# A channel shuffle in 24-row tiles: stores issued in turn by ScalarE and GpSimd, copies on VectorE alone, small tiles at both ends

## The chip, the cores and the metric

One core of a Trainium2 chip. The experiments ran in five sessions, on chips 1, 3, 12 and 13, and each ratio is against the kernel before as run in the same session. The time is device microseconds (us) of one execution, and medians are given with the lowest and highest of all executions of that kernel on the chip at hand.

## The reference

The input `x` is float32 of shape 16 x 64 x 64 x 256. The 256 channels of each pixel are 8 groups of 32, and the result has the two axes exchanged: output channel `i*8 + g` is input channel `g*32 + i`. Nothing is computed; 67.11 MB are read and 67.11 MB written.

```python
x = x.reshape(batch, h, w, groups, channels_per_group)
x = x.transpose(0, 1, 2, 4, 3)
x = x.reshape(batch, h, w, c)
```

## The kernel before

The pixels are a list of 65,536 rows of 256 floats. A tile holds 24 rows on each of 128 partitions (24 KB a partition, 3 MB in all); there are 21 such tiles and one of 8 rows. Each is loaded from SyncE's queue, permuted inside each partition by two strided copies (first half of the rows on VectorE, second on ScalarE), and stored from ScalarE's queue. Four input and four output buffers let the stages overlap; a scheduler decides the order on each engine.

```python
_SIZES = [24] * 21 + [8]
_IN_BUFS = 4
_OUT_BUFS = 4
_SHARES = (("vector", 1), ("scalar", 1))
# ... cut: rows() takes q rows for each of 128 partitions; permute() is one strided copy
    first = 0
    for q in _SIZES:
        in_tile = in_pool.tile([P, biggest * c], F32, name="in_tile")
        nc.sync.dma_start(out=in_tile[:, : q * c], in_=rows(x_flat, first, q))
        out_tile = out_pool.tile([P, biggest * c], F32, name="out_tile")
        at, total = 0, sum(n for _, n in _SHARES)
        for k, (engine, n) in enumerate(_SHARES):
            # ... cut: the engine's share of the rows, at to upto
                permute(engine, out_tile[:, cols], in_tile[:, cols])
        nc.scalar.dma_start(out=rows(out_flat, first, q), in_=out_tile[:, : q * c])
        first += P * q
```

Of the kernel before, what the change touches and what calls it, by code (L numbers as in the profile page):

```python
# [1 line left out]

# [4 lines left out]


F32 = mybir.dt.float32
P = 128  # L10

_SIZES = [24] * 21 + [8]
_IN_BUFS = 4
_OUT_BUFS = 4

_SHARES = (("vector", 1), ("scalar", 1))


@with_exitstack
def kernel(  # L20
    ctx: ExitStack,
    tc: tile.TileContext,
    x: bass.AP,
    groups: bass.AP,
    out: bass.AP,
):
    nc = tc.nc
    b, h, w, c = x.shape
    G = int(groups)
    CPG = c // G  # L30
    assert G * CPG == c
    assert sum(_SIZES) * P == b * h * w
    biggest = max(_SIZES)

    x_flat = x.rearrange("b h w c -> (b h w c)")
    out_flat = out.rearrange("b h w c -> (b h w c)")

    in_pool = ctx.enter_context(tc.tile_pool(name="in_pool", bufs=_IN_BUFS))
    out_pool = ctx.enter_context(tc.tile_pool(name="out_pool", bufs=_OUT_BUFS))

    def rows(flat, first, q):

        return flat[first * c : (first + P * q) * c].rearrange("(p f) -> p f", p=P)

    def permute(engine, dst, src):
        src = src.rearrange("p (i g j) -> p i j g", g=G, j=CPG)
        dst = dst.rearrange("p (i j g) -> p i j g", j=CPG, g=G)
        if engine == "scalar":
            nc.scalar.copy(out=dst, in_=src)  # L49
        else:  # L50
            getattr(nc, engine).tensor_copy(out=dst, in_=src)  # L51

    first = 0
    for q in _SIZES:
        in_tile = in_pool.tile([P, biggest * c], F32, name="in_tile")
        nc.sync.dma_start(out=in_tile[:, : q * c], in_=rows(x_flat, first, q))
        out_tile = out_pool.tile([P, biggest * c], F32, name="out_tile")
        at, total = 0, sum(n for _, n in _SHARES)
        for k, (engine, n) in enumerate(_SHARES):
            last = k == len(_SHARES) - 1  # L60
            upto = q if last else min(q, at + -(-q * n // total))
            if upto > at:
                cols = slice(at * c, upto * c)
                permute(engine, out_tile[:, cols], in_tile[:, cols])
            at = upto
        nc.scalar.dma_start(out=rows(out_flat, first, q), in_=out_tile[:, : q * c])  # L66
        first += P * q


# [1 line left out]
_INS = ['x', 'groups']  # L71
_OUTS = [((16, 64, 64, 256), 'float32')]

_NUMBERS = {'groups': 8}


# [26 lines left out]
```

## Time and profile before

| | before |
|---|---|
| time, median (lowest to highest) | 317.53 us (317.53 to 317.59, 3 runs) |
| span of the profiled run | 316.0 us |
| DMA engines' time: loads, stores | 49.8%, 49.3% |
| start of one tile's copy to the next, 103.62 to 292.64 us | 14.54 us (13 steps) |

The page of the profile opens with the busy time of each engine. In its strip each digit is the busy share, in tenths, of one fortieth of the span (7.9 us here); the GB/s line says what the DMA engines moved in it. Then come the DMA queues (q1 is SyncE's, q10 ScalarE's) and the costliest groups of instructions, with the idle time before them and who ended it.

```profile
span 316.0 us, 236 instructions
DVE 65.3 (21%) x22; ACT 118.9 (38%) x23; POOL 0.2 (0%) x4
...
DMA  8999999999999999999999999999999999999996
GB/s 302 439 395 426 426 445 432 420 442 439 417 439 445 417 436 442 426 426 445 426 423 445 439 414 442 442 417 439 442 421 432 442 420 432 442 429 429 421 446 291
...
q1 hardware_dynamic: 3168, 67.11, 49.8%
q10 hardware_dynamic: 3168, 67.11, 49.3%
...
L49 ACT COPY out_tile<-in_tile 128x3072 f32<-128x3072 f32 (+1 forms) x22 | 117.7, 5348 | 184.6 <-DMA in_tile<-in_x_dram 184.6
L51 DVE COPY out_tile<-in_tile 128x3072 f32<-128x3072 f32 (+1 forms) x22 | 65.3, 2968 | 238.3 <-DMA in_tile<-in_x_dram 238.3
```

The two queues add up to 99.1% of the time of all sixteen DMA engines, and both copying engines spend most of the span waiting for loads. The kernel is bound by DMA; only the first and the last slice are short. The windows view of the same run says it by stretch. Its columns are the stretch, its length, the busy us of VectorE, ScalarE and GpSimd (with their instructions), the granted clock, the DMA share and the GB/s; rows left out are marked by dots.

```profile
100.00:150.00 50.00, 11.83 (x4) 19.12 (x4) 0.00 (x0) 1.00 1.00 433
200.00:250.00 50.00, 9.90 (x4) 17.29 (x4) 0.00 (x0) 1.00 1.00 432
...
300.00:308.00 8.00, 1.09 (x1) 1.94 (x1) 0.00 (x0) 1.00 1.03 443
308.00:314.00 6.00, 0.00 (x0) 0.00 (x0) 0.00 (x0) 1.00 0.90 382
314.00:316.00 2.00, 0.00 (x0) 0.00 (x0) 0.00 (x0) 1.00 0.01 4
```

So about 433 GB/s is held to 308 us, and 382 from there to 314. 134.22 MB at 433 GB/s are 310.0 us. The timeline shows why the end is full: when the last small load lands at 302.35, two stores (4 MB, 9.7 us of DMA) are still to be made.

```profile
292.64 5.43 ACT L49 COPY out_tile<-in_tile 128x3072 f32<-128x3072 f32 x1 [9.11 <-DMA in_tile<-in_x_dram]
...
302.35 1.94 ACT L49 COPY out_tile<-in_tile 128x1024 f32<-128x1024 f32 x1 [4.29 <-DMA in_tile<-in_x_dram]
302.41 2.25 ACTq L66 DMA_DIRECT2D out_dram<-out_tile  x2
```

### The profile page before, as it was taken

The page shows a single profiled execution, that of the slowest core. Times are in us where ns is not written, and L with a number is a line of the kernel's source. Part 1 is how long each engine was busy: PE and PEld are TensorE (multiplying, and loading weights), DVE is VectorE, ACT ScalarE, POOL GpSimd, SP SyncE. Part 2 cuts the span into 40 slices and gives each one's busy share as a digit, 9 for nine tenths or more (in the row PEclk, how much of TensorE's full clock was granted, in tenths as well). Part 3 has the DMA queues.
Part 4 walks back from the last instruction along what each step waited for, and adds up shares of the span by engine and source line. Part 5 has one row for each costly group of instructions (what it writes and reads, how often), then busy time and mean ns, then how long its engine had stood idle before and what let it go on. Part 6 is the DMA issues. An engine that isn't in the chain of part 4 may idle for free.

```text
span 316.0 us, 236 instructions
## 1 busy us (share of the span) xinstructions
DVE 65.3 (21%) x22; ACT 118.9 (38%) x23; POOL 0.2 (0%) x4
## 2 busy tenths in 40 slices
DVE  0440321303030303113030303031220303030310
ACT  1681624425160606243351606061533426060620
POOL 0000000000000000000000000000000000000000
DMA  8999999999999999999999999999999999999996
GB/s 302 439 395 426 426 445 432 420 442 439 417 439 445 417 436 442 426 426 445 426 423 445 439 414 442 442 417 439 442 421 432 442 420 432 442 429 429 421 446 291
DMA packets 6337, 134.23 MB, mean 425 GB/s; under 512 B 704, under 2 KB 704, under 8 KB 704
## 3 DMA queue, kind: packets, MB, share of 16 engines
q1 hardware_dynamic: 3168, 67.11, 49.8%
q10 hardware_dynamic: 3168, 67.11, 49.3%
q14 instruction: 1, 0.01, 0.0%
HBM read 67.11 MB, written 67.11 MB: 425 GB/s over the span
## 4 chain that ended last, share of the span: by engine, by line
another core or an unknown queue 43%; DMA 32%; ACT 20%; ACTq 1%; issue 0%
DMA in_tile<-in_x_dram 32%; ACT out_tile L49 20%; ACTq L66 1%; ACTq L49 0%
## 5 line engine op out<-in xcount | busy, mean ns | idle before, releaser
L49 ACT COPY out_tile<-in_tile 128x3072 f32<-128x3072 f32 (+1 forms) x22 | 117.7, 5348 | 184.6 <-DMA in_tile<-in_x_dram 184.6
L51 DVE COPY out_tile<-in_tile 128x3072 f32<-128x3072 f32 (+1 forms) x22 | 65.3, 2968 | 238.3 <-DMA in_tile<-in_x_dram 238.3
L49 ACT ACT_TABLE_LOAD x1 | 1.3, 1283 | 0.7 <-PEq L84 0.7
L84 POOL MEMSET const-bfloat16-1.0<- 128x1 bf16 x1 | 0.1, 102 | 0.0
L84 POOL MEMSET const-uint8-127<- 128x1 uint8 x1 | 0.1, 102 | 0.0
L84 POOL MEMSET const-float32-1.0<- 128x1 f32 x1 | 0.1, 99 | 0.0
L84 POOL MEMSET const-float32-0.0<- 128x1 f32 x1 | 0.1, 98 | 0.2 <-issue 0.2
## 6 DMA issues: line engine op xcount, KB each, us to landing
in_tile<-in_x_dram SPq DMA_DIRECT2D x21, 3072.0 KB, 52.6
out_dram<-out_tile ACTq DMA_DIRECT2D x21, 3072.0 KB, 20.2
in_tile<-in_x_dram SPq DMA_DIRECT2D x1, 1024.0 KB, 47.9
out_dram<-out_tile ACTq DMA_DIRECT2D x1, 1024.0 KB, 10.4
```

Of the source, the lines that this page charges most:

```text
L49: nc.scalar.copy(out=dst, in_=src)
L51: getattr(nc, engine).tensor_copy(out=dst, in_=src)
L66: nc.scalar.dma_start(out=rows(out_flat, first, q), in_=out_tile[:, : q * c])
L84: nc = _bacc.Bacc("TRN2", target_bir_lowering=False, num_devices=1)
```

## The change

The intent: take the copies off ScalarE so that it need only issue stores; issue each store right after its copy, from two engines in turn; start and end with small tiles so that the pipeline fills and drains faster.

```diff
-_SIZES = [24] * 21 + [8]
+_SIZES = [8] + [24] * 20 + [8, 8, 8]
-_SHARES = (("vector", 1), ("scalar", 1))
+_SHARES = (("vector", 1),)
...
+    ctx.enter_context(tc.manual_schedule(engines=None))
     first = 0
-    for q in _SIZES:
+    for t, q in enumerate(_SIZES):
...
-        nc.scalar.dma_start(out=rows(out_flat, first, q), in_=out_tile[:, : q * c])
+        storer = (nc.scalar, nc.gpsimd)[t % 2]
+        storer.dma_start(out=rows(out_flat, first, q), in_=out_tile[:, : q * c])
```

## The prediction

> **What bounds the kernel now.** The 16 DMA engines. The strip of slices shows DMA at 9 tenths or more in 38 of 40 slices; the queue part gives 49.8% of the engines' span to loads and 49.3% to stores, 99.1% together. In steady state the timeline's copies start every 14.55 us; one tile loads and stores 6.29 MB, so 432.5 GB/s. 134.2 MB at that rate is 310.3 us, against a span of 316.0. Only about 5.7 us is left to win, all at the ends: slice 1 moved 302 GB/s and slice 40 moved 291. VectorE is 21% busy, ScalarE 38%; the groups by line show both waiting for loads (238 and 185 us). The chain of waits names ScalarE for 20%, but DMA never ran dry under it.
>
> **The change, costed.**
> 1. Copies. ScalarE loses 22 copies (5.51 us per 12 rows), VectorE doubles: 12 rows took 3.06 us, so 24 rows about 6.0 us (estimate), 8 rows 2.0. About 130 us busy in all, 6.0 of each 14.55. Off the critical path: 0.
> 2. Program order. Now stores go out in pairs: store 20 was issued at 302.4 us though its copies ended at 298.1. Afterwards each goes right after its copy. In steady state DMA has work anyway: 0.
> 3. Two store queues. The Trainium skill, "DMA: Bandwidth & Descriptors", section "Issuing engines are not separate DMA queues", says all issuers share the same 16 engines. At 99.1% busy this brings no bandwidth. I expect 14.5 to 14.6 us per tile again. A GpSimd store will start 0.5 to 2 us later than a ScalarE one (a guess; this trace has no GpSimd DMA). "SBUF — State Buffer" (box on the "DVE blocks DMA" trap) says descriptor writing is locked out while VectorE copies in a two-port mode. Here VectorE is idle 8.5 us of each 14.55, and a store is issued just when its copy has ended, so little should be lost.
> 4. Small first tile. The first store goes near 8.5 us, not 16.8. But four loads already fill DMA then: 0.
> 5. Three small last tiles. Here I expect a loss. Now the last small load took 9.7 us (292.6 to 302.35) beside a large store, four times its own 2.4 us: small rows share badly. At its landing about 4.2 MB of stores were still to go, and covered the last copy. Afterwards three small loads crawl beside two store queues that drain the backlog early. After the last landing come copy 2.0, issue 1.2 to 2.5, transfer 2.4, completion about 1.3 us, with only the store before (2.4 us) to cover copy and issue. DMA idle at the end: 1.5 to 4 us more.
>
> Sum: +1.5 to +4 us, perhaps one more if GpSimd's queue is costly: 317.5 becomes about 319.8 us, range 316.3 to 324.0. Faster by over 2% would need 311.2 us, which leaves no ends at all: 1%. Slower by over 2% needs the GpSimd queue to lower the steady rate: 11%. Within 2%: 88%.
>
> **What would show it.** Copy spacing 14.5 to 14.6 us; VectorE near 130 us busy; first slices as full as now; fewer GB/s in the last two slices, with a gap between the last load's landing and the last store, which GpSimd issues; the first GpSimd store landing later than a ScalarE one.
>
> **What would make it wrong.** GpSimd descriptors smaller than the rows (many more packets) or uneven over engines, lowering the rate below 430 GB/s; descriptor writing that waits for VectorE; or, to the good side, last stores still backed up when the last load lands, so that the end is no longer than now.

## The result

| | before | after |
|---|---|---|
| time, median (lowest to highest), 6 runs each | 317.56 us (317.53 to 317.80) | 326.15 us (325.18 to 327.88) |
| ratio after / before, 95% interval | | 1.0271 (1.0242 to 1.0300) |
| span of the profiled run | 316.0 us | 326.1 us |
| VectorE busy | 65.3 us | 121.8 us |
| start of one 24-row copy to the next, mean of 13 | 14.54 us | 14.97 us (100.35 to 294.95) |

A ratio is the mean time of one kernel's fast runs over that of the other's fast runs of the same rounds, so it is not quite the ratio of the medians quoted. The change is slower by 2.7%. The profiled execution after is the slowest of its six (327.88 us), so its span overstates the difference a little; the spread among runs, 2.7 us against 0.3 before, is itself new.

The page after, with the lines that answer to those of before (q0 is GpSimd's software queue):

```profile
span 326.1 us, 175 instructions
DVE 121.8 (37%) x24; POOL 6.7 (2%) x16
...
DMA  8999999999999999999999999999999999999953
GB/s 322 394 425 434 425 434 425 434 431 431 425 431 434 428 434 428 428 422 428 422 410 431 434 434 434 434 431 431 431 428 419 431 425 431 431 410 388 411 250 133
...
q1 hardware_dynamic: 3456, 67.11, 48.5%
q10 hardware_dynamic: 1728, 33.56, 24.2%
q0 software_dynamic: 1728, 33.56, 24.1%
...
L51 DVE COPY out_tile<-in_tile 128x6144 f32<-128x6144 f32 (+1 forms) x24 | 121.8, 5077 | 198.6 <-DMA in_tile<-in_x_dram 198.6
L68 POOL DMA_DIRECT2D out_dram<-out_tile x12 | 6.5, 543 | 314.3 <-DVE out_tile L51 314.3
```

VectorE still mostly waits for loads: it has not become the bound. The software queue moved as many packets as ScalarE's (1,728 each, the same bytes), so the rows were not cut smaller. What changed is the last two slices, 250 and 133 GB/s where before had 446 and 291, and a little less than 433 in many others. The windows view after has no column for ScalarE, which runs no copies any more:

```profile
100.00:150.00 50.00, 22.79 (x4) 1.06 (x2) 1.00 1.00 429
200.00:250.00 50.00, 18.39 (x4) 0.53 (x1) 1.00 1.00 428
250.00:290.00 40.00, 15.69 (x3) 1.06 (x2) 1.00 1.00 425
...
300.00:308.00 8.00, 2.71 (x3) 0.53 (x1) 1.00 0.92 390
308.00:314.00 6.00, 2.00 (x1) 0.00 (x0) 1.00 0.97 408
314.00:318.00 4.00, 0.00 (x0) 0.00 (x0) 1.00 0.20 86
318.00:322.00 4.00, 2.02 (x1) 0.53 (x1) 1.00 0.10 41
322.00:326.00 4.00, 0.00 (x0) 0.00 (x0) 1.00 0.56 229
```

From 314 to 322 us the DMA share is 0.2 and then 0.1: about three, then fewer than two of sixteen engines at work on average. The timeline of that stretch shows what everybody was waiting for:

```profile
294.95 5.68 DVE L51 COPY out_tile<-in_tile 128x6144 f32<-128x6144 f32 x1 [8.01 <-DMA in_tile<-in_x_dram]
...
302.80 2.05 DVE L51 COPY out_tile<-in_tile 128x2048 f32<-128x2048 f32 x1 [2.17 <-DMA in_tile<-in_x_dram]
...
307.97 2.02 DVE L51 COPY out_tile<-in_tile 128x2048 f32<-128x2048 f32 x1 [3.12 <-DMA in_tile<-in_x_dram]
318.38 2.02 DVE L51 COPY out_tile<-in_tile 128x2048 f32<-128x2048 f32 x1 [8.38 <-DMA in_tile<-in_x_dram]
320.69 0.53 POOL L68 DMA_DIRECT2D out_dram<-out_tile  x1 [15.01 <-DVE out_tile L51]
```

The last load, 1 MB, landed 10.4 us after the one ahead of it, though DMA was nearly idle for the last four of those. Only then could the last copy and the last store be made, with nothing to cover them.

### Why a load lands late while DMA is idle

A DMA of 128 partitions is spread over all sixteen engines, and each raises the semaphore once when its own share is done (704 landings for the 44 DMAs before). The trace keeps these sixteen times. Their spread, first to last, says how far apart the engines are:

```
one load's sixteen landings (us)   first    median   last     spread
before, last load                  300.77   301.66   302.33    1.56
after, first tile                    5.03     5.42     5.64    0.62
after, fifth load                   53.72    54.23    55.43    1.71
after, copied at 158.81            154.96   155.37   158.68    3.72
after, copied at 281.23            268.07   269.31   281.10   13.02
after, last load                   295.69   298.43   318.25   22.56
```

Before, no DMA had a spread over 1.6 us anywhere. After, it grows all through the run, and one engine finished its share of the last load 20 us later than the median engine. A copy waits for the sixteenth. Nine of the engines stay together: of the sixteen landings of the load copied at 302.80, nine lie between 287.8 and 288.1 us, six between 290.6 and 294.8, and the last at 302.7.

The trace also has each packet (here one row block of one partition, 24 KB) with queue, start and duration, but not its engine. A packet nearly always starts 3 or 4 ns before the end of another; joining them that way gives sixteen chains of about 396 records before and 432 after, that is, the engines (where two end at the same moment a join can be wrong, so small counts mean little). The end of the run on some engines, in order of time: L a load packet, S one of ScalarE's stores, G one of GpSimd's.

```
before, from 285 us
 engine a   SLSLSLSSLSLSLLSLSLSLSLSSSSSSSSSSSSSSSSSSSS
 engine b   SLSLSLSSLSLSLLSLSLSLSLSSSSSSSSSSSSSSSSSSSS
after, from 288 us
 engine a   LLLLLLLLLLLLGLGLGLGGGGGSSSSSSSSGGGGGGGGSSSSSSSSGGGGGGGG
 engine b   LLLLLLLLLLLLLGLGLGGGGGGSSSSSSSSGGGGGGGGSSSSSSSSGGGGGGGG
 the last   SLLLGLGGLGLGLGLGLGLLLLLLLLLSLSLSSLSGLSGLSGLSGLGLSGLSGLSGSSSSSGGGGGGGG
```

Before, the engines do the same things in the same order. After, half of them have finished their loads by 298.4 us and have only stores left (a and b are two of these), while the last one still has some twenty load packets to do, and from about the middle on it takes turns L S G: with two store queues filled, a load of that engine gets one turn in three. The Trainium skill, "DMA: Bandwidth & Descriptors", section "Queues, rings and completion order", says that each DMA engine goes round the queues for which it has work, a packet at a time; these sequences agree, with one record of 8 or 24 KB to a turn.

A plain account per engine, in the two profiled runs (mean of sixteen, from the first packet of all to the last):

```
                    busy      idle     of busy: over the usual time per packet, after 16 us
before              312.0     0.7      0.8
after               314.3     8.4      2.6
```

"The usual time" is 912 ns for 24 KB and 309 ns for 8 KB, which nearly all packets took. After, 4.5% of the packets took over 20 ns longer (after the first 16 us, up to about twice as long), before 0.9%. So of the 10.1 us between the two spans, 7.7 us are engines left idle at the end and 2.3 us longer busy time. The strings above tie the idle part to engines that are out of step; why packets take longer they do not tell.

The mean hides how the two parts hang together. Taken engine by engine in the same chains, up to 288 us, the engine that is last has done 10.0 us less of packet work than the median engine (each packet counted at its usual time), and its packets have taken 10.2 us longer than the median engine's; the next three are behind by 4.0, 3.1 and 2.5 us, with 4.2, 3.1 and 1.9 us of longer packets. So by then an engine is behind by about as much as its own packets ran over. The turns of one in three at the end then double the 10 us for its last load, and the others wait for it.

### The profile page after: what moved, and what is told of

Same layout as the page of the kernel before. It is cut to its first block, busy times and chain, and to the rows that moved or that the text cites. A ratio compares the mean times of both kernels' runs of the same rounds, so it can differ in the third digit from the quotient of the medians.

```text
span 326.1 us, 175 instructions
## 1 busy us (share of the span) xinstructions
DVE 121.8 (37%) x24; POOL 6.7 (2%) x16
## 3 DMA queue, kind: packets, MB, share of 16 engines
q10 hardware_dynamic: 1728, 33.56, 24.2%
q0 software_dynamic: 1728, 33.56, 24.1%
## 4 chain that ended last, share of the span: by engine, by line
issue 38%; another core or an unknown queue 25%; DVE 18%; DMA 16%; POOL 1%; POOLq 0%; DVEq 0%
DVE out_tile L51 18%; DMA in_tile<-in_x_dram 16%; POOL out_dram L68 1%; POOLq L100 0%; DVEq L51 0%; POOLq L68 0%
## 5 line engine op out<-in xcount | busy, mean ns | idle before, releaser
L51 DVE COPY out_tile<-in_tile 128x6144 f32<-128x6144 f32 (+1 forms) x24 | 121.8, 5077 | 198.6 <-DMA in_tile<-in_x_dram 198.6
L68 POOL DMA_DIRECT2D out_dram<-out_tile x12 | 6.5, 543 | 314.3 <-DVE out_tile L51 314.3
```

Source lines behind the costliest of these rows:

```text
L51: getattr(nc, engine).tensor_copy(out=dst, in_=src)
L68: storer.dma_start(out=rows(out_flat, first, q), in_=out_tile[:, : q * c])
```

## The experiments

Fifteen kernels were run, each in 3 rounds or (f1) 5. In the expectations, T1 is the theory that two store queues side by side drive the engines out of step, T2 that the software queue does so as such, T3 that the small tiles or the order do. I give one table, then each run. "Spread" is the largest of any DMA in the profiled run; "long" is busy time over the usual packet time, and "idle" is as above, both per engine in us.

| run | queues and turns | median us (lowest to highest) | ratio (95%) | spread | long | idle |
|---|---|---|---|---|---|---|
| before | 2, even | 317.5 to 317.7 in all sessions | 1 | 1.6 | 0.8 | 0.7 |
| after | 3, stores in turn | 326.15 (325.18 to 327.88) | 1.0271 (1.0242, 1.0300) | 22.6 | 2.6 | 8.4 |
| e1_scalar_only | 2, even | 318.43 (318.30 to 318.64) | 1.0022 (1.0007, 1.0037) | 4.0 | 0.4 | 1.3 |
| e2_gpsimd_only | 2, even, software | 319.12 (318.56 to 320.01) | 1.0046 (1.0026, 1.0066) | 6.6 | 0.4 | 1.8 |
| e3_old_sizes | 3, stores in turn | 323.69 (321.74 to 326.96) | 1.0171 (1.0117, 1.0224) | 12.6 | 2.3 | 4.1 |
| e4_before_two_storers | 3, stores in turn | 324.33 (323.59 to 326.94) | 1.0222 (1.0179, 1.0265) | 8.6 | 6.2 | 1.7 |
| f1_copies_and_order | 2, even | 317.38 (317.12 to 317.44) | 0.9992 (0.9980, 1.0005) | 1.3 | 0.9 | 0.6 |
| f2_loads_on_two | 3, loads in turn | 319.33 (318.29 to 320.43) | 1.0066 (1.0043, 1.0090) | 3.0 | 1.1 | 0.9 |
| f3_one_in_four | 3, at times | 318.29 (317.42 to 325.70) | 1.0013 (0.9989, 1.0036) | 9.6 | 1.3 | 1.9 |
| f4_mixed_queues | 2, even | 317.38 (317.36 to 317.56) | 0.9995 (0.9981, 1.0008) | 0.7 | 1.1 | 0.4 |
| g1_halves | 3, even | 319.25 (319.14 to 319.39) | 1.0051 (1.0036, 1.0066) | 0.7 | 1.1 | 0.8 |
| g2_far_apart | 3, stores in turn | 324.12 (321.67 to 325.66) | 1.0197 (1.0146, 1.0247) | 14.2 | 5.4 | 4.1 |
| h1_stores_in_halves | 2, uneven | 323.40 (321.00 to 324.61) | 1.0157 (1.0106, 1.0209) | 12.8 | 3.9 | 3.3 |
| h2_loads_in_halves | 2, uneven | 325.51 (323.76 to 328.00) | 1.0251 (1.0195, 1.0307) | 8.1 | 2.9 | 4.6 |
| i1_changed_halves | 3, even | 320.71 (320.28 to 323.20) | 1.0090 (1.0073, 1.0107) | 9.2 | 0.5 | 4.4 |

The medians are of all runs. In e3 one run (326.96) and in f3 one (325.70) count as slow, being over 1.5% above the fastest; the ratios leave them out, and the medians without them are 322.77 and 317.45 us. g3 and g4, which give a wrong result, are not in the table.

### e1_scalar_only: the change without GpSimd

```diff
-        storer = (nc.scalar, nc.gpsimd)[t % 2]
+        storer = nc.scalar
```

> The changed kernel with every store on ScalarE: no software queue, two queues in all; the sizes, VectorE's copies and the program order stay. If the GpSimd queue is the cause (T1: as a third queue beside a second store queue; T2: because it is a software queue), the sixteen engines stay in step: landings of one load spread by under 2 us throughout, packets of 24 KB at 912 ns, the steady rate 433 GB/s, and what is left is the cost of the small last tiles as I predicted it, 318 to 320 us. If the small tiles or the program order are the cause (T3), it stays at 324 to 327 us and the spread still grows above 10 us.

Measured: 318.43 us. Over 7 of the 8.6 us go away with this one line, and 24 KB packets took 912 to 914 ns on every engine (means, after the first 16 us). The spread stayed at 2.4 us or less except at the very end (4.0). T3 falls as the main cause. The small tiles, the copies and the order together cost 0.2%, less than I had predicted for the small tiles. The timeline shows the small loads in question: their copies started 9.7 and 5.0 us apart, but the last one at 309.8, not 318.4.

```profile
295.11 2.04 DVE L51 COPY out_tile<-in_tile 128x2048 f32<-128x2048 f32 x1 [3.95 <-DMA in_tile<-in_x_dram]
304.83 2.06 DVE L51 COPY out_tile<-in_tile 128x2048 f32<-128x2048 f32 x1 [7.68 <-DMA in_tile<-in_x_dram]
309.80 2.02 DVE L51 COPY out_tile<-in_tile 128x2048 f32<-128x2048 f32 x1 [2.92 <-DMA in_tile<-in_x_dram]
```

### e2_gpsimd_only: the change without ScalarE's stores

```diff
-        storer = (nc.scalar, nc.gpsimd)[t % 2]
+        storer = nc.gpsimd
```

> The changed kernel with every store on GpSimd: two queues, one of them software. T1 (three queues with two store queues side by side drive the engines out of step): as with ScalarE alone within 1 us, spread under 2 us, no slow packets, plus at most 1 us for the later last store. T2 (the software queue itself upsets the engines, by its descriptors or their ring): as slow as the changed kernel or slower, 326 to 335 us, with the spread growing and single engines with mean packet times over 930 ns.

Measured: 319.12 us, 0.7 us over ScalarE alone, with packets at 912 to 913 ns on all sixteen engines (as in e1) and a spread of 2.2 us through the middle (6.6 once, at the end). T2 falls: a software queue with all of the stores does no harm. It takes the two together.

### e3_old_sizes: the change without the small tiles

```diff
-_SIZES = [8] + [24] * 20 + [8, 8, 8]
+_SIZES = [24] * 21 + [8]
```

> The changed kernel with the sizes of before (21 tiles of 24 rows, then one of 8); two storers, VectorE's copies and program order stay. T1 and T2: the engines still drift apart (spread over 10 us near the end, slowest engine over 930 ns a packet), and the time is 321 to 327 us. T3 (the small tiles at the ends are the cause): 316 to 318 us and no drift.

Measured: 323.69 us, between 321.74 and 326.96; 322.77 without the slow run. The drift is there without the small tiles (spread 12.6 us). With fast runs alone the small tiles make the loss larger by some 3 us at most (326.15 against 322.77, from two sessions).

### e4_before_two_storers: the kernel before with two storers

```diff
-        nc.scalar.dma_start(out=rows(out_flat, first, q), in_=out_tile[:, : q * c])
+        (nc.scalar, nc.gpsimd)[t % 2].dma_start(out=rows(out_flat, first, q), in_=out_tile[:, : q * c])
```

> The kernel before with one thing changed: stores alternate between ScalarE and GpSimd (copies split over VectorE and ScalarE, scheduler order, old sizes). T1 and T2: the drift is there, 320 to 327 us. If it needs VectorE's long copies [...] or the program order: at most 318.5 us, no drift.

Measured: 324.33 us, 2.2% slower, by this line alone in the otherwise old kernel. Here most of the loss is longer packets (6.2 us per engine) and the rest idle engines; the page's strip shows it spread over the whole span, not only at the end.

```profile
DMA  8999999999999999999999999999999999999996
GB/s 314 427 390 430 436 439 427 439 427 433 421 414 439 418 418 408 430 414 424 421 421 439 411 427 430 430 411 424 430 424 424 424 433 405 430 418 424 413 385 279
```

The DMA line still reads 9 everywhere: busy, and slower. Only the GB/s line tells.

### f1, f2, f3, f4: which part of two storers

f1 leaves the copies and the order of the change alone (old sizes, ScalarE stores). f2 and f3 start from f1:

```diff
 # f2_loads_on_two
-        nc.sync.dma_start(out=in_tile[:, : q * c], in_=rows(x_flat, first, q))
+        (nc.sync, nc.gpsimd)[t % 2].dma_start(out=in_tile[:, : q * c], in_=rows(x_flat, first, q))
 # f3_one_in_four
-        storer = nc.scalar
+        storer = nc.gpsimd if t % 4 == 3 else nc.scalar
```

f4 has no GpSimd either; loads are issued three tiles ahead, and the two hardware queues exchange roles with each tile:

```diff
 # f4_mixed_queues
+        loader = (nc.sync, nc.scalar)[t % 2]
+        storer = (nc.scalar, nc.sync)[t % 2]
```

> The kernel before with only VectorE's copies and the program order of the change: sizes of before, every store on ScalarE. My prediction gave both 0 us: 316.8 to 318.2 us, engines in step (spread of one DMA's landings under 3 us). If long VectorE copies or in-order stores do harm by themselves, over 319 us. It is also the nearest candidate for a version better than both: perhaps 0.5 us under before, as the last store need not wait for the next copy to start.

Measured: 317.38 us, ratio 0.9992, in step (1.3 us). The prediction's 0 us for the copies and for the order holds. It is no better than before within the interval.

> Three queues again, but the loads are what alternates (SyncE and GpSimd); every store is on ScalarE. If any third bulk queue beside two others drives the engines apart (theory U1), the landings spread over 5 us, mean packet time over 915 ns, 320 to 328 us. If it needs two store queues side by side (U2), at most 318.5 us, spread under 3 us.

Measured: 319.33 us, and neither theory's numbers. Slower by 0.7%, but the spread stayed at 3.0 us and few packets were long. A third queue on the loads' side is much milder than on the stores' side. It is not that the turns were even: joined into chains as above, the trace has rounds of three packets from three queues, two loads to a store, at some 70 of 100 packets from 30 to 100 us, and at 27 of 100 from 30 to 290 us (6 of 100 in the changed kernel). All sixteen engines take them alike, and in those 70 us no spread was over 2.3 us. So uneven turns alone do not drive engines apart; what else it takes is not shown.

> Only each fourth store goes to GpSimd, sizes of before. A dose: if the harm comes each time a third queue is filled beside the other two, about a half of what the run with alternate stores and old sizes lost (that was 6 us; now 2 to 4 us, 319.5 to 321.5). If the engines, once out of step, do not come back, the full loss, 322 us or more. If rare software stores are harmless, at most 318.3 us.

Measured: three of four executions gave 317.42 to 319.13; the fourth, 325.70, counts as slow and is left out of the ratio; whether it was the drift can't be told, as it has no trace. The spread reached 9.6 us in the profiled run (319.13 us). The dose I expected, 2 to 4 us, did not show: at a quarter of the stores the loss of the fast runs is within noise, though the engines still drift (7.0 us between 98 and 288 us).

> No GpSimd: the two hardware queues (SyncE, ScalarE) carry loads and stores in turn each, loads issued three tiles ahead, sizes of before. If the trouble is three queues or a software queue beside a hardware one, the engines stay in step: spread under 3 us, 317 to 318.5 us. If what keeps the engines in step is that one queue has loads alone and one has stores alone (strict turn of load and store on each engine), the spread grows here too and the time is over 320 us.

Measured: 317.38 us, spread 0.7 us, the best step of all. It is not necessary that one queue carries loads alone.

### g1_halves: three queues, even turns

Theory V1 (turns): when two store queues hold work an engine gives stores two turns in three, otherwise one in two; this happens at different moments on each engine, so they lose step. Rivals: V2, two store streams hinder each other; V3, they do so when they write near each other. From the change with old sizes:

```diff
-        storer.dma_start(out=rows(out_flat, first, q), in_=out_tile[:, : q * c])
+        half = q // 2 * c
+        place = rows(out_flat, first, q)
+        nc.scalar.dma_start(out=place[:, :half], in_=out_tile[:, :half])
+        nc.gpsimd.dma_start(out=place[:, half:], in_=out_tile[:, half : q * c])
```

> The changed kernel with old sizes, each tile's store cut in two halves of 12 rows, one on ScalarE and one on GpSimd at the same moment. Theory V1 (turns): with whole stores in turn, stores get two of three turns of a DMA engine while both store queues hold something and one of two otherwise, at other moments on each engine, and so the engines lose step. Here a round is one load packet of 24 KB and two store packets of 12 KB, even again: landings of a load spread under 4 us, 317 to 319 us. Theory V2 (two store streams hinder each other wherever they meet, or a software queue beside a hardware store queue does): as bad as whole stores in turn, slow packets all through, 321 us or more.

Measured: 319.25 us, 0.25 over the range given. Both store queues are now filled at once for every tile, one of them software, and the engines stay in step better than before (spread 0.7 us through the run), with no long packets. Against e3 (whole stores in turn; 322.77 us for its fast runs), 3.5 us are won back by cutting each store over the same two queues. The windows view has 432 GB/s up to 308 us and 416 up to 314:

```profile
200.00:250.00 50.00, 17.25 (x4) 1.60 (x3) 1.00 1.01 432
...
300.00:308.00 8.00, 2.02 (x1) 0.55 (x2) 1.00 1.01 432
308.00:314.00 6.00, 0.00 (x0) 0.00 (x0) 1.00 0.99 416
```

The remaining 1.6 us over before fit the smaller packets: a 12 KB packet took 460 ns, 4 more than half of 912, and each engine has 336 of them, 1.3 us (an estimate from these numbers).

### g2_far_apart: the two stores in different halves of the output

```diff
-    for t, q in enumerate(_SIZES):
+    order = [t // 2 + 11 * (t % 2) for t in range(len(_SIZES) - 1)] + [len(_SIZES) - 1]
+    for t, k in enumerate(order):
+        q, first = _SIZES[k], P * 24 * k
```

> The changed kernel with old sizes, but ScalarE's tiles lie in the first half of the tensor and GpSimd's in the second, so the two stores in flight write places some 34 MB apart instead of 3 MB. V1 (turns): no difference, 321 to 327 us, spread over 5 us. If the slow packets come of two stores near each other in DRAM (V3): slow packets under 1 in 100, at most 319 us.

Measured: 324.12 us, spread 14.2 us, as bad as e3. V3 falls.

### g3_stores_two and g4_stores_one: stores without loads

Both give a wrong result: one tile is loaded and copied once and stored to all 22 places.

```diff
 # g3; g4 has storer = nc.scalar
+    in_tile = in_pool.tile([P, biggest * c], F32, name="in_tile")
+    nc.sync.dma_start(out=in_tile, in_=rows(x_flat, 0, biggest))
+    out_tile = out_pool.tile([P, biggest * c], F32, name="out_tile")
+    permute("vector", out_tile, in_tile)
     first = 0
     for t, q in enumerate(_SIZES):
# ... cut: the load and the copy of each tile are taken out of the loop
         storer = (nc.scalar, nc.gpsimd)[t % 2]
         storer.dma_start(out=rows(out_flat, first, q), in_=out_tile[:, : q * c])
```

> Wrong on purpose: one tile is loaded and copied once and then stored to all 22 places, alternately by ScalarE and GpSimd, with no loads beside them. 67.1 MB at 433 GB/s are 155 us, plus some 20 us for the head. V2: against the same with ScalarE alone it is 3% slower or more, with slow packets (over 930 ns) in more than 3 of 100. V1: equal within 1%, as there is no third party to lose its turn to.

> Wrong on purpose: the same with ScalarE storing alone, as the yardstick: about 175 us, all packets at 912 ns.

Measured: 178.18 us (177.96 to 178.28) and 176.93 us (176.69 to 177.14): 0.7% apart, within V1's 1%. My yardstick of 912 ns was a little off: without loads a 24 KB store packet took 920 and 923 ns on average in the two queues of g3 and 918 in the one of g4, and as many packets were over 20 ns above 912 in one as in the other (204 and 203 of 2,944). So the slow packets that V2 expected were there with one store queue too, and tell nothing for it. Two store streams by themselves do not hinder each other; V2 falls in its plain form.

### h1_stores_in_halves and h2_loads_in_halves: uneven turns without GpSimd

From f1. W1: uneven turns between loads and stores are enough. W2: it takes three queues.

```diff
 # h1; half and place as in g1
-        storer.dma_start(out=rows(out_flat, first, q), in_=out_tile[:, : q * c])
+        nc.scalar.dma_start(out=place[:, :half], in_=out_tile[:, :half])
+        nc.scalar.dma_start(out=place[:, half:], in_=out_tile[:, half : q * c])
 # h2; place is rows(x_flat, first, q)
-        nc.sync.dma_start(out=in_tile[:, : q * c], in_=rows(x_flat, first, q))
+        nc.sync.dma_start(out=in_tile[:, :half], in_=place[:, :half])
+        nc.sync.dma_start(out=in_tile[:, half : q * c], in_=place[:, half:])
```

> VectorE's copies, program order, old sizes, all stores on ScalarE, each as two stores of 12 rows one after the other: stores get one third of an engine while both queues hold something. If uneven turns are enough (W1): spread over 4 us, packets over 930 ns in more than 1 of 100, 320 us or more. If it takes three queues (W2): spread under 3 us, 318 to 319.5 us (1.4 us of it because a 12 KB packet took 460 ns, more than half of 912).

Measured: 323.40 us, spread up to 12.8 us, 3.4% of packets long. W1. The pieces are those of g1, which kept step within 0.7 us, so it is not the cutting as such.

> The same with whole stores and each load as two loads of 12 rows one after the other, both on SyncE: stores get two thirds of an engine while both queues hold something, the share that two store queues had in the changed kernel. W1: as above, 320 us or more with a growing spread. W2: 318 to 319.5 us, in step.

Measured: 325.51 us, spread 8.1 us. W1 again, and nearly the whole loss of the change (ratio 1.0251 against 1.0271), with two hardware queues, whole stores on one engine, old sizes. The windows view shows the same two marks, less than 433 in the middle and a hole near the end:

```profile
200.00:250.00 50.00, 18.83 (x4) 0.00 (x0) 1.00 1.00 425
...
300.00:308.00 8.00, 3.29 (x1) 0.00 (x0) 1.00 0.85 361
308.00:314.00 6.00, 4.30 (x2) 0.00 (x0) 1.00 0.50 211
314.00:318.00 4.00, 0.00 (x0) 0.00 (x0) 1.00 1.14 492
```

The turn goes by the packet, not by the byte: in that run an engine's chain reads L S L S with L of 12 KB and S of 24 KB while both queues are filled, then long runs of L alone.

### i1_changed_halves: the whole change with even turns

The edit of g1 in the changed kernel as it is.

> The changed kernel as it is, with its sizes, both storers, VectorE's copies and program order; each tile's store is cut in two halves, one on each storer at the same moment. If the uneven turns are the whole loss: 319.5 to 321 us (318.4 with ScalarE alone, plus 1.4 for 12 KB packets, plus GpSimd's later start at the very end), engines in step, spread under 2 us. If small tiles beside two store queues cost by themselves: 322 us or more.

Measured: 320.71 us, inside the range expected of uneven turns; 5.4 us below the changed kernel. The step was not as good as expected: the spread held at 3.3 us from 98 to 288 us instead of under 2, without growing, and rose to 9.2 at the small tiles. Of the 2.3 us over e1, 1.3 are the smaller packets (as in g1) and 0.7 what GpSimd cost over ScalarE when alone; 0.3 are left, within the scatter of the runs (an estimate: that these parts add up was not tested). The profiled execution is the slowest of the five (323.20), so the 4.4 us of idle in the table are more than usual. So 5.4 of the 8.6 us go away when the turns are made even.

## Why the prediction was wrong

The prediction said 319.8 us, 316.3 to 324.0, and gave "slower by over 2%" 11%. It was 326.15 us, 2.7% slower.

**The step that failed: 3, two store queues.** It read "At 99.1% busy this brings no bandwidth. I expect 14.5 to 14.6 us per tile again." The first sentence is right, the second does not follow from it. Measured: 14.97 us from copy to copy, 3.0% more, though all engines together still moved 425 to 430 GB/s from 100 to 290 us against 433, about 1% less. I treated the sixteen engines as one pipe that shares its rate. They are sixteen, each with its own order of packets (the strings above), and a load has landed only when the slowest of them is done: that one was 10 us behind the median engine by 288 us, by packets that took longer. The runs show:

- The second store queue is the cause: added alone to the kernel before it costs 2.2% (e4); taken out of the changed kernel, 7.7 us go (e1). This is shown.
- Neither the software queue (e2), nor two store streams as such (g3 against g4), nor their places in DRAM (g2), nor VectorE's copies and the order (f1) does it.
- Uneven turns between loads and stores were enough with two hardware queues and no GpSimd (h1, h2), and even turns over the same three queues take most of it away (g1, i1). They are not always enough: f2 had more of them than the changed kernel, the other way round, and lost only 0.7%. In the trace of the changed kernel it shows as a spread of one load's landings that grows from 0.6 to 22.6 us, and at the end as the L S G turns of the engine that is last.

**Step 5, the small last tiles: mechanism right, size dependent on step 3.** A last load landing late, then copy, issue and store with nothing to cover them: that is what the end of the timeline shows. The term "with only the store before (2.4 us) to cover copy and issue" made it 1.5 to 4 us. With one store queue the small tiles cost about 0.9 us (e1 against f1, each measured from its own session's before: 318.43 from 317.72, and 317.38 from 317.57). With two that drifted, an engine's lag of 20 us came on top, and 7.7 us more of idle per engine in the profiled run. I had seen that small rows "share badly" beside a large store, four times slower, and drew from it only the end, not that unequal turns have an effect in the whole run.

**Right:** step 1 (VectorE 121.8 us busy, a little under the 130 I estimated since 24 rows took 5.7 us; off the critical path, f1); step 2 (0, f1); step 4, on the whole (the first slices are as full as before: 322 and 394 against 302 and 439); packets of GpSimd as large as ScalarE's; no waiting of descriptor writing for VectorE that could be seen (the first GpSimd store was issued 0.3 us after its copy's end). The later start of a GpSimd store, guessed at 0.5 to 2 us, was 0.7 us for the first store (from issue to its first packet 4.1 us in e1, 4.8 in e2) and 0.3 us for the last (0.84 and 1.10). On descriptor writing the Trainium skill, "SBUF — State Buffer", box on the "DVE blocks DMA" trap, was not put to the test: the stores are issued when VectorE is idle, and no run here shows such a wait.

**Of the warnings at the end** I named "uneven over engines", but meant the software queue's spreading of packets. Packets were spread evenly, a mean of 96 (ScalarE), 192 (loads) and 96 (GpSimd) to an engine, and eight of each large store in the strings above; their order was not the same.

**What stays open.** Why a packet takes longer than 912 ns at all when engines are out of step: long packets came in all three queues, before 0.9% of packets, 7.7% in e4. What they collide with, the trace does not say. An engine's lag is the extra time of its own long packets, but what starts them, and why a few engines get most of them, is not shown. Also open is why uneven turns in favour of loads cost only 0.7% in f2 and keep the engines within 3 us, while in h1, where they also favour loads, they cost 1.6%. No version beat the kernel before: f1 and f4 are equal to it within their intervals.

## What to carry to other kernels

When DMA is the bound and full, look at how the queues take turns, not only at how many bytes they carry. In this kernel it did best to give each engine one load packet for as many store bytes, in queues that fill and empty together, and to leave it at two queues, as two kept the engines busy. A second storing engine gained nothing here and cost 2.2% (e4). Read the spread of one DMA's sixteen landings, early and late in the run: a spread that grows means that the engines have lost step, and that each load is as late as the last of them, though the busy share still reads 9 in 10. Then look at that engine by itself: a mean over sixteen engines had 2.6 us of long packets where the last one had over 10.

## What the Trainium skill lacked or had wrong

- "DMA: Bandwidth & Descriptors", section "Issuing engines are not separate DMA queues", says that spreading DMAs over issuing engines only saves issue time. It lacks that it can cost: 2.2% in e4, where the one change is a second storer.
- The same page, section "Queues, rings and completion order", has engines switch queues after a packet of typically 9 to 17 descriptors. With rows of 24 KB they switched after every record of the trace, and a turn did not depend on its bytes (12 KB against 24 KB in h2); how many descriptors a record holds the trace does not show. The page lacks what can follow: engines whose queues take unequal turns can drift apart, up to 22.6 us between the first and the last landing of one load (but only 3.0 in f2).
- The same page, section "Latency and other measured facts", gives as its best guess, not certain, that the software queue's descriptor rings make two DMA engines slower. With all stores in that queue (e2) the mean 24 KB packet was 912 to 913 ns on all sixteen engines, as far as the joined chains tell.
- No page that I looked up has the spread of a DMA's sixteen semaphore landings as something to read in a trace. Between 98 and 288 us the largest spread was 8.1 to 13.0 us in the six kernels that were over 1.5% slower, 7.0 in f3, and at most 3.3 in all others.
